# Softmax over 16384 rows: row maxima taken out of the main path, and two late loads moved to another queue

## The chip, the cores and the metric

The kernel runs on one core of a Trainium2 chip. The metric is device time in microseconds (us). The profile's span runs from the first to the last instruction and is some 1.3 to 1.6 us shorter than the device time.

## The reference, cut to what matters

```python
x: float32 [16, 1024, 512], standard normal
x_scaled = x / 2.0
exp_x = exp(x_scaled - max(x_scaled, axis=-1))
out = exp_x / sum(exp_x, axis=-1)
```

That is 16384 softmaxes over 512 values. Input and output are 33.55 MB each. A "row" below is one 512-value row of each of the 128 partitions, 0.262 MB; there are 128 of them.

## The kernel before

Ten tiles of 3, 7, 13 and seven times 15 rows share an SBUF arena of 98 rows, so tiles 8 and 9 must wait until earlier tiles are stored.

```python
# loads: tile 0 on SyncE's queue, tiles 1 to 7 on ScalarE's, all issued at once
nc.sync.dma_start(out=sb(0), in_=dram(xf, 0))                   # t == 0
for p, q, lo, hi in ((0, P, 0, r), (0, 126, r, r + 1), (126, P, r, r + 1)):   # t == 1
    nc.scalar.dma_start(out=sb(t)[p:q, lo:hi], in_=dram(xf, t)[p:q, lo:hi])
...
# VectorE, chunk k (3 to 5 rows): maxima, and two chunks behind them the division
nc.vector.reduce_max(out=stats[...], in_=arena[...], negate=True)._wait_ge(ld[t], ...)
nc.vector.reciprocal(out=recip[...], in_=stats[...])._wait_ge(s_exp, k + 1)
nc.vector.tensor_mul(...)                       # tiles 1 to 3: one per chunk
nc.vector.tensor_scalar_mul(...)                # other tiles: one per row
...
# ScalarE, per row: waits for the chunk's maxima
nc.scalar.activation(out=arena[:, a + r], in_=arena[:, a + r], func=Exp,
    bias=stats[:, b + r : b + r + 1], scale=0.5, accum_out=stats[:, b + r : b + r + 1])
... # after the exponentials of tiles 4 and 5: the late loads, on ScalarE's queue
nc.scalar.wait_ge(*need[u]); nc.scalar.dma_start(out=sb(u), in_=dram(xf, u))   # u = 8, 9
...
# SyncE: the stores, in order
for t in range(len(tiles)):
    nc.sync.wait_ge(s_mul, last_chunk[t] + 1)
    nc.sync.dma_start(out=dram(of, t), in_=sb(t))
```

## Time and profile before

| | before |
|---|---|
| time, median of 3 runs | 160.1 us (160.06 to 160.21) |
| span of the profiled run | 158.6 us |
| VectorE busy | 131.4 us, 83% |
| ScalarE busy | 94.4 us, 60% |
| two DMA queues, share of 16 engines | 50.6% and 48.5% |

Besides the lines that the prediction shows, these are the page's costliest groups of the kernel before. The columns are line, engine, operation, operands, count; then busy us and mean ns; then the idle time ahead of them and what ended it.

```profile
L118 DVE TENSOR_REDUCE stats<-arena 128x5 f32<-128x2560 f32 (+2 forms) x27 | 72.2, 2676 | 14.6 <-DMA arena<-in_x_dram 14.6
L176 ACT ACTIVATE arena<-arena,stats 128x512 f32<-128x512 f32 x68 | 48.2, 710 | 23.4 <-DVE stats L118 23.4
L138 DVE TENSOR_SCALAR arena<-arena,recip 128x512 f32<-128x512 f32 x93 | 38.6, 482 | 0.7
L131 DVE TENSOR_TENSOR arena<-arena,recip 128x2560 f32<-128x2560 f32 (+2 forms) x8 | 19.9, 2491 | 0.3
```

The first line is the whole cost of the row maxima: more than half of VectorE's busy time. The second shows ScalarE waiting 23.4 us for them.

### The profile page before, as it was taken

How to read it: one execution, taken by the hardware profiler on the slowest of the kernel's cores; microseconds unless marked ns; L12 is line 12 of the kernel's file. 1: busy time of each engine (PE TensorE's matmuls, PEld its weight loads, DVE VectorE, ACT ScalarE, POOL GpSimd, SP SyncE). 2: the span in 40 equal slices, each digit the busy share in tenths (PEclk: the TensorE clock that was granted, in tenths of full speed). 3: DMA queues.
4: the chain of work that ended last, by engine and by line, in shares of the span. 5: the costliest groups of instructions: out<-in, count | busy, mean ns of one | idle time of the engine just before them, and what ended most of it. 6: DMA issues, size and time to landing. Idle time of an engine off the chain costs nothing.

```text
span 158.6 us, 621 instructions
## 1 busy us (share of the span) xinstructions
DVE 131.4 (83%) x155; ACT 94.4 (60%) x257; POOL 0.2 (0%) x4
## 2 busy tenths in 40 slices
DVE  0466799999999999999999999996999389999000
ACT  0369197736874594669738797666566809763000
POOL 0000000000000000000000000000000000000000
DMA  7999999999999999999999999999999999999996
GB/s 268 449 373 430 414 431 466 435 407 399 466 443 389 434 463 448 418 444 426 442 426 434 426 426 442 426 441 411 457 395 472 395 473 395 472 395 465 395 472 263
DMA packets 3026, 67.13 MB, mean 423 GB/s; under 512 B 336, under 2 KB 336, under 8 KB 720
## 3 DMA queue, kind: packets, MB, share of 16 engines
q1 hardware_dynamic: 1584, 34.34, 50.6%
q10 hardware_dynamic: 1440, 32.77, 48.5%
q14 instruction: 2, 0.02, 0.0%
HBM read 33.55 MB, written 33.55 MB: 423 GB/s over the span
## 4 chain that ended last, share of the span: by engine, by line
DMA 52%; DVE 38%; issue 0%
DMA arena<-in_x_dram 38%; DVE stats L118 18%; DMA out_dram<-arena 14%; DVE arena L131 13%; DVE arena L138 7%; DVE recip L127 1%
## 5 line engine op out<-in xcount | busy, mean ns | idle before, releaser
L118 DVE TENSOR_REDUCE stats<-arena 128x5 f32<-128x2560 f32 (+2 forms) x27 | 72.2, 2676 | 14.6 <-DMA arena<-in_x_dram 14.6
L176 ACT ACTIVATE arena<-arena,stats 128x512 f32<-128x512 f32 x68 | 48.2, 710 | 23.4 <-DVE stats L118 23.4
L211 ACT ACTIVATE arena<-arena,stats x60 | 42.5, 710 | 20.7 <-ACTq L203 20.7
L138 DVE TENSOR_SCALAR arena<-arena,recip 128x512 f32<-128x512 f32 x93 | 38.6, 482 | 0.7
L131 DVE TENSOR_TENSOR arena<-arena,recip 128x2560 f32<-128x2560 f32 (+2 forms) x8 | 19.9, 2491 | 0.3
L176 ACT ACTIVATION_READ_ACCUMULATOR arena<-arena,stats 128x1 f32 x68 | 12.7, 187 | 0.0
L211 ACT ACTIVATION_READ_ACCUMULATOR arena<-arena,stats x60 | 11.2, 187 | 0.0
L127 DVE RECIPROCAL recip<-stats 128x5 f32<-128x5 f32 (+2 forms) x27 | 4.8, 177 | 0.0
L171 ACT ACT_TABLE_LOAD x1 | 1.3, 1283 | 5.7 <-issue 5.7
L252 POOL MEMSET const-bfloat16-1.0<- 128x1 bf16 x1 | 0.1, 101 | 0.0
L252 POOL MEMSET const-uint8-127<- 128x1 uint8 x1 | 0.1, 101 | 0.0
L252 POOL MEMSET const-float32-0.0<- 128x1 f32 x1 | 0.1, 98 | 0.2 <-issue 0.2
L252 POOL MEMSET const-float32-1.0<- 128x1 f32 x1 | 0.1, 98 | 0.0
## 6 DMA issues: line engine op xcount, KB each, us to landing
arena<-in_x_dram ACTq DMA_DIRECT2D x7, 3840.0 KB, 46.6
out_dram<-arena SPq DMA_DIRECT2D x7, 3840.0 KB, 22.7
arena<-in_x_dram ACTq DMA_DIRECT2D x1, 3328.0 KB, 14.3
out_dram<-arena SPq DMA_DIRECT2D x1, 3328.0 KB, 21.1
out_dram<-arena SPq DMA_DIRECT2D x1, 1792.0 KB, 18.2
arena<-in_x_dram ACTq DMA_DIRECT2D x1, 1536.0 KB
arena<-in_x_dram SPq DMA_DIRECT2D x1, 768.0 KB, 6.2
out_dram<-arena SPq DMA_DIRECT2D x1, 768.0 KB, 15.8
```

What stands on the lines that cost most here:

```text
L118: nc.vector.reduce_max(out=stats[:, b : b + c], in_=arena[:, a : a + c], axis=mybir.AxisListType.X, negate=True,)._wait_ge(ld[t], 48 if t ...
L127: nc.vector.reciprocal(out=recip[:, b : b + c], in_=stats[:, b : b + c])._wait_ge(s_exp, k + 1).then_inc(s_rec, 1)
L131: nc.vector.tensor_mul(out=arena[:, a : a + c], in0=arena[:, a : a + c], in1=recip[:, b : b + c].unsqueeze(2).to_broadcast([P, c, D]),)._w ...
L138: ins = nc.vector.tensor_scalar_mul(out=arena[:, a + r], in0=arena[:, a + r], scalar1=recip[:, b + r : b + r + 1],)
L171: nc.scalar.preload_act_table(mybir.ActivationFunctionType.Exp)
L176: ins = nc.scalar.activation(out=arena[:, a + r], in_=arena[:, a + r], func=mybir.ActivationFunctionType.Exp, bias=stats[:, b + r : b + r ...
L211: ins = nc.scalar.activation(out=data, in_=data, func=mybir.ActivationFunctionType.Exp, bias=stat, scale=0.5, accum_out=stat,)
L252: nc = _bacc.Bacc("TRN2", target_bir_lowering=False, num_devices=1)
```

## The change

The intent is to relieve VectorE: exponentials of x/2 without the maximum subtracted are safe for ordinary data, so the main path drops the maxima, checks at its end that all 16384 sums lie between 1 and 1e30, and otherwise computes everything again in a general path with maxima, whose DMAs GpSimd issues. The two late loads go to SyncE's queue, between stores. Two smaller parts go along: the divisions become 18 products of up to ten rows, and ScalarE's loop takes 105 rows instead of 60.

```diff
-        nc.vector.reduce_max(out=stats[:, b : b + c], in_=arena[:, a : a + c], negate=True, ...)
...
                 ins = nc.scalar.activation(
-                    out=arena[:, a + r], in_=arena[:, a + r], func=Exp,
-                    bias=stats[:, b + r : b + r + 1], scale=0.5,
-                    accum_out=stats[:, b + r : b + r + 1],
+                    out=arena[:, b], in_=arena[:, b], func=Exp, scale=0.5,
+                    accum_out=stats[:, b : b + 1],
                 )
...
-        for r in range(c):
-            ins = nc.vector.tensor_scalar_mul(...)
+            nc.vector.tensor_mul(...)          # 18 in all, over up to 10 rows
...
-                nc.scalar.wait_ge(*need[u])
-                nc.scalar.dma_start(out=sb(u), in_=dram(xf, u)).then_inc(ld[u], 16)
...
+        for t in (0, 1, 2, 3):
+            store(nc.sync, t)
+        for t, then in ((8, (4,)), (9, (5, 6, 7, 8, 9))):
+            nc.sync.wait_ge(s_home[t], landings(LATE[t]))
+            load(nc.sync, t)
+            for u in then:
+                store(nc.sync, u)
...
+        nc.vector.tensor_scalar(out=inside[:, :], in0=stats[:, :], scalar1=LO, scalar2=HI, ...)
+        ...                                    # compare, count, 1x1 matmul, flag
+        rounds(nc.vector, vector)              # general path, skipped when the flag says so
+        rounds(nc.scalar, scalar)
+        rounds(nc.gpsimd, gpsimd, n_rows // G)
```

More of the change, by code (lines that the diff above doesn't have):

```diff
@@ L6 @@
 from concourse._compat import with_exitstack
-PLAN = [
-    ([3], 0), ([4, 3], 3), ([5, 4, 4], 10), ([5] * 3, 23), ([5] * 3, 38), ([5] * 3, 53),
-    ([5] * 3, 68), ([5] * 3, 83), ([5] * 3, 0), ([5] * 3, 15),
+TILES = [
+    (3, 0), (7, 3), (13, 10), (15, 23), (15, 38), (15, 53), (15, 68), (15, 83), (15, 0), (15, 15),
 ]
+LATE = {8: (0, 1, 2), 9: (3,)}
 ARENA = 98
-LAG = 2
+HEAD = [3, 4, 3, 5, 4, 4]
+E = 5
 SPREAD = 1
-AFTER = {8: 4, 9: 5}
-FUSED = {1, 2, 3}
-LOOP = 6
-E = 5
+LO, HI = 1.0, 1.0e30
+G = 8
 @with_exitstack
@@ L38 @@
     fp32 = mybir.dt.float32
+    Exp = mybir.ActivationFunctionType.Exp
+    Alu = mybir.AluOpType
     xf = x.flatten_outer_dims()
@@ L44 @@
     n_rows = N // P
-    assert sum(sum(c) for c, _ in PLAN) == n_rows
+    assert sum(r for r, _ in TILES) == n_rows
     arena = nc.alloc_sbuf_tensor("arena", (P, ARENA, D), fp32)
@@ L50 @@
     recip = nc.alloc_sbuf_tensor("recip", (P, n_rows), fp32)
-    tiles, chunks, base = [], [], 0
-    for t, (cs, at) in enumerate(PLAN):
-        r = sum(cs)
+    inside = nc.alloc_sbuf_tensor("inside", (P, n_rows), fp32)
+    count = nc.alloc_sbuf_tensor("count", (P, 1), fp32)
+    ones = nc.alloc_sbuf_tensor("ones", (P, 1), fp32)
+    flag = nc.alloc_sbuf_tensor("flag", (1, 1), mybir.dt.int32)
+    g_max = nc.alloc_sbuf_tensor("g_max", (P, G), fp32)
+    g_sum = nc.alloc_sbuf_tensor("g_sum", (P, G), fp32)
+    total = nc.alloc_psum_tensor("total", (1, 1), fp32)
+    tiles, base = [], 0
+    for r, at in TILES:
+        assert at == base % ARENA
         tiles.append((base, r, at))
-        o = 0
-        for c in cs:
-            chunks.append((t, base + o, c, at + o))
-            o += c
         base += r
-    last_chunk = {c[0]: k for k, c in enumerate(chunks)}
     def dram(ap, t):
@@ L71, in sb @@
         return arena[:, at : at + r, :]
-    behind = {}
-    for t, (_, r, at) in enumerate(tiles):
-        for u in range(t):
-            _, ru, au = tiles[u]
-            if at < au + ru and au < at + r:
-                behind.setdefault(t, []).append(u)
-    ld = [nc.alloc_semaphore(f"ld{t}") for t in range(len(tiles))]
-    awaited = sorted({u for us in behind.values() for u in us})
-    st, need = {}, {}
-    for t in sorted(behind):
-        new = [u for u in behind[t] if u not in st]
-        sem = nc.alloc_semaphore(f"st{t}")
-        st.update({u: sem for u in new})
-        need[t] = (sem, 16 * len(new))
+    straight = sum(HEAD)
+    sizes = HEAD + [E] * ((n_rows - straight) // E)
+    starts = [sum(sizes[:k]) for k in range(len(sizes))]
+    assert sum(sizes) == n_rows
+    owner = [max(t for t, (b, _, _) in enumerate(tiles) if b <= s) for s in starts]
+    assert all(s + c <= sum(tiles[t][:2]) for s, c, t in zip(starts, sizes, owner))
+    pairs = []
+    for k, t in enumerate(owner):
+        if pairs and len(pairs[-1]) == 1 and owner[pairs[-1][0]] == t:
+            pairs[-1].append(k)
+        else:
+            pairs.append([k])
+    upto = [1 + max(j for j, ks in enumerate(pairs) if owner[ks[0]] == t) for t in range(len(tiles))]
+    ld = [nc.alloc_semaphore(f"ld{t}") for t in range(len(tiles))]
+    s_home = {t: nc.alloc_semaphore(f"s_home{t}") for t in LATE}
     s_end = nc.alloc_semaphore("s_end")
-    s_max = nc.alloc_semaphore("s_max")
     s_exp = nc.alloc_semaphore("s_exp")
@@ L96 @@
     s_mul = nc.alloc_semaphore("s_mul")
-    def issue_loads(begin, end):
-        for t in range(begin, end):
-            if t in behind:
-                continue
-            if t == 0:
-                nc.sync.dma_start(out=sb(t), in_=dram(xf, t)).then_inc(ld[t], 16)
-            elif t == SPREAD:
-                r = tiles[t][1] - 1
-                for p, q, lo, hi in ((0, P, 0, r), (0, 126, r, r + 1), (126, P, r, r + 1)):
-                    nc.scalar.dma_start(
-                        out=sb(t)[p:q, lo:hi], in_=dram(xf, t)[p:q, lo:hi]
-                    ).then_inc(ld[t], 16)
-            else:
-                nc.scalar.dma_start(out=sb(t), in_=dram(xf, t)).then_inc(ld[t], 16)
@@ L116, in do_max @@
-    def do_max(k):
-        t, b, c, a = chunks[k]
-        nc.vector.reduce_max(
-            out=stats[:, b : b + c],
-            in_=arena[:, a : a + c],
-            axis=mybir.AxisListType.X,
-            negate=True,
-        )._wait_ge(ld[t], 48 if t == SPREAD else 16).then_inc(s_max, 1)
-    def do_mul(k):
-        t, b, c, a = chunks[k]
-        nc.vector.reciprocal(
-            out=recip[:, b : b + c], in_=stats[:, b : b + c]
-        )._wait_ge(s_exp, k + 1).then_inc(s_rec, 1)
-        if t in FUSED:
+    s_ones = nc.alloc_semaphore("s_ones")
@@ new lines, with load @@
+    s_cnt = nc.alloc_semaphore("s_cnt")
+    s_tot = nc.alloc_semaphore("s_tot")
+    s_flag = nc.alloc_semaphore("s_flag")
+    g_ld = nc.alloc_semaphore("g_ld")
+    g_go = nc.alloc_semaphore("g_go")
+    g_st = nc.alloc_semaphore("g_st")
+    g_neg = nc.alloc_semaphore("g_neg")
+    g_exp = nc.alloc_semaphore("g_exp")
+    g_rec = nc.alloc_semaphore("g_rec")
+    g_mul = nc.alloc_semaphore("g_mul")
+    def load(eng, t):
+        r = tiles[t][1]
+        parts = [(0, P, 0, r)]
+        if t == SPREAD:
+            parts = [(0, P, 0, r - 1), (0, 126, r - 1, r), (126, P, r - 1, r)]
+        for p, q, lo, hi in parts:
+            eng.dma_start(
+                out=sb(t)[p:q, lo:hi], in_=dram(xf, t)[p:q, lo:hi]
+            ).then_inc(ld[t], 16)
@@ new lines, with landings, store @@
+    stored_by = {u: s_home[t] for t, us in LATE.items() for u in us}
+    for t, (_, r, at) in enumerate(tiles):
+        over = {u for u, (_, ru, au) in enumerate(tiles[:t]) if at < au + ru and au < at + r}
+        assert over <= {u for v, us in LATE.items() if v <= t for u in us}
+    def landings(ts):
+        return 16 * len(list(ts))
+    at_end = landings(t for t in range(len(tiles)) if t not in stored_by)
+    def store(eng, t):
+        eng.wait_ge(s_mul, upto[t])
+        eng.dma_start(out=dram(of, t), in_=sb(t)).then_inc(stored_by.get(t, s_end), 16)
@@ new lines, in take, with rounds, early, loads @@
+    def take(eng, sem, n):
+        eng.wait_ge(sem, n).then_inc(sem, -n)
+    def rounds(eng, body, step=1):
+        last = n_rows // G
+        i = eng.alloc_register("tile")
+        eng.wait_ge(s_flag, 1)
+        eng.reg_load(i, flag[0:1, 0:1])
+        with eng.While(lambda: eng.snap(i, min_val=0, max_val=last) < last):
+            body(eng.snap(i, min_val=0, max_val=last - 1))
+            eng.reg_add(i, i, step)
+    def early():
+        load(nc.sync, 0)
+        load(nc.scalar, 1)
+    def loads():
+        for t in range(2, min(LATE)):
+            load(nc.scalar, t)
@@ L131, in do_mul, with program @@
+    def program():
+        nc.vector.memset(ones[:, :], 1.0).then_inc(s_ones, 1)
+        for j, ks in enumerate(pairs):
+            b, c = starts[ks[0]], sum(sizes[k] for k in ks)
+            a = b % ARENA
+            nc.vector.reciprocal(
+                out=recip[:, b : b + c], in_=stats[:, b : b + c]
+            )._wait_ge(s_exp, ks[-1] + 1).then_inc(s_rec, 1)
             nc.vector.tensor_mul(
@@ L134, in do_mul @@
                 in1=recip[:, b : b + c].unsqueeze(2).to_broadcast([P, c, D]),
-            )._wait_ge(s_rec, k + 1).then_inc(s_mul, 1)
-            return
-        for r in range(c):
-            ins = nc.vector.tensor_scalar_mul(
-                out=arena[:, a + r],
-                in0=arena[:, a + r],
-                scalar1=recip[:, b + r : b + r + 1],
-            )
-            if r == 0:
-                ins._wait_ge(s_rec, k + 1)
-        ins.then_inc(s_mul, 1)
-    def compute_and_store():
-        for k in range(len(chunks) + LAG):
-            if k < len(chunks):
-                do_max(k)
-            if k >= LAG:
-                do_mul(k - LAG)
-        for t in range(len(tiles)):
-            nc.sync.wait_ge(s_mul, last_chunk[t] + 1)
-            nc.sync.dma_start(out=dram(of, t), in_=sb(t)).then_inc(
-                st[t] if t in awaited else s_end, 16
-            )
-        nc.sync.wait_ge(s_end, 16 * (len(tiles) - len(awaited)))
-        straight = [k for k, c in enumerate(chunks) if c[0] < LOOP]
-        loop = [k for k, c in enumerate(chunks) if c[0] >= LOOP]
-        for k in loop:
-            nc.tensor.wait_ge(s_max, k + 1).then_inc(s_go, 1)
-        nc.scalar.preload_act_table(mybir.ActivationFunctionType.Exp)
-        late = sorted(behind)
-        for k in straight:
-            t, b, c, a = chunks[k]
-            for r in range(c):
-                ins = nc.scalar.activation(
-                    out=arena[:, a + r],
-                    in_=arena[:, a + r],
-                    func=mybir.ActivationFunctionType.Exp,
-                    bias=stats[:, b + r : b + r + 1],
-                    scale=0.5,
-                    accum_out=stats[:, b + r : b + r + 1],
-                )
-                if r == 0:
-                    ins._wait_ge(s_max, k + 1)
@@ new lines, in program @@
+            )._wait_ge(s_rec, j + 1).then_inc(s_mul, 1)
+        nc.vector.tensor_scalar(
+            out=inside[:, :], in0=stats[:, :], scalar1=LO, scalar2=HI,
+            op0=Alu.max, op1=Alu.min,
+        ).then_inc(s_cnt, 1)
+        nc.vector.tensor_tensor(
+            out=inside[:, :], in0=inside[:, :], in1=stats[:, :], op=Alu.is_equal
+        )._wait_ge(s_cnt, 1).then_inc(s_cnt, 1)
+        nc.vector.reduce_sum(
+            out=count[:, :], in_=inside[:, :], axis=mybir.AxisListType.X
+        )._wait_ge(s_cnt, 2).then_inc(s_cnt, 1)
@@ new lines, in program @@
+        nc.vector.tensor_scalar(
+            out=flag[:, :], in0=total[:, :], scalar1=float(N), scalar2=float(n_rows // G),
+            op0=Alu.is_ge, op1=Alu.mult,
+        )._wait_ge(s_tot, 1).then_inc(s_flag, 1)
+        for t in range(len(tiles)):
+            nc.tensor.wait_ge(ld[t], 48 if t == SPREAD else 16).then_inc(s_go, owner.count(t))
+        nc.tensor.wait_ge(s_ones, 1)
+        nc.tensor.matmul(
+            total[:, :], lhsT=count[:, :], rhs=ones[:, :], start=True, stop=True
+        )._wait_ge(s_cnt, 3).then_inc(s_tot, 1)
@@ L186, in compute_and_store @@
+        nc.scalar.preload_act_table(Exp)
+        for k, c in enumerate(HEAD):
+            take(nc.scalar, s_go, 1)
+            for b in range(starts[k], starts[k] + c):
+                ins = nc.scalar.activation(
+                    out=arena[:, b], in_=arena[:, b], func=Exp, scale=0.5,
+                    accum_out=stats[:, b : b + 1],
+                )
             ins.then_inc(s_exp, 1)
-            while late and last_chunk[AFTER[late[0]]] <= k:
-                u = late.pop(0)
-                nc.scalar.wait_ge(*need[u])
-                nc.scalar.dma_start(out=sb(u), in_=dram(xf, u)).then_inc(ld[u], 16)
@@ L191, in compute_and_store @@
-        assert not late
-        first = chunks[loop[0]][1]
-        assert all(
-            c == E and b == first + j * E and a == b % ARENA
-            for j, (_, b, c, a) in enumerate(chunks[k] for k in loop)
-        )
-        row = nc.scalar.alloc_register("row")
+        exponentials(straight, n_rows)
+        for t in (0, 1, 2, 3):
[5 more added lines that the diff above has]
+                store(nc.sync, u)
@@ new lines, in program, with vector @@
+        x_g = xf.rearrange("(t p r) d -> t p r d", p=P, r=G)
+        o_g = of.rearrange("(t p r) d -> t p r d", p=P, r=G)
+        data = arena[:, 0:G]
+        def vector(i):
+            take(nc.vector, g_go, 1)
+            nc.vector.reduce_max(
+                out=g_max[:, :], in_=data, axis=mybir.AxisListType.X, negate=True
+            ).then_inc(g_rec, 1)
+            take(nc.vector, g_rec, 1)
+            nc.vector.tensor_scalar_mul(
+                out=g_max[:, :], in0=g_max[:, :], scalar1=0.5
+            ).then_inc(g_neg, 1)
+            take(nc.vector, g_exp, 1)
+            nc.vector.reciprocal(out=g_sum[:, :], in_=g_sum[:, :]).then_inc(g_rec, 1)
+            take(nc.vector, g_rec, 1)
+            nc.vector.tensor_mul(
+                out=data, in0=data, in1=g_sum[:, :].unsqueeze(2).to_broadcast([P, G, D])
+            ).then_inc(g_mul, 1)
@@ new lines, in scalar, with gpsimd @@
+        def scalar(i):
+            take(nc.scalar, g_neg, 1)
+            for r in range(G):
+                ins = nc.scalar.activation(
+                    out=arena[:, r], in_=arena[:, r], func=Exp, scale=0.5,
+                    bias=g_max[:, r : r + 1], accum_out=g_sum[:, r : r + 1],
+                )
+            ins.then_inc(g_exp, 1)
+        def gpsimd(_):
+            nc.gpsimd.wait_ge(s_end, at_end)
+            for i in range(n_rows // G):
+                nc.gpsimd.dma_start(out=data, in_=x_g[i]).then_inc(g_ld, 16)
+                nc.gpsimd.wait_ge(g_ld, 16 * (i + 1)).then_inc(g_go, 1)
+                take(nc.gpsimd, g_mul, 1)
+                nc.gpsimd.dma_start(out=o_g[i], in_=data).then_inc(g_st, 16)
+                nc.gpsimd.wait_ge(g_st, 16 * (i + 1))
@@ L200, in compute_and_store, with exponentials @@
+        rounds(nc.vector, vector)
+        rounds(nc.scalar, scalar)
+        rounds(nc.gpsimd, gpsimd, n_rows // G)
+        nc.sync.wait_ge(s_end, at_end)
+    def exponentials(first, end):
+        row = nc.scalar.alloc_register(f"row{first}")
         nc.scalar.reg_mov(row, first)
-        with nc.scalar.While(lambda: nc.scalar.snap(row, min_val=first, max_val=n_rows) < n_rows):
-            now = nc.scalar.snap(row, min_val=first, max_val=n_rows - E)
-            nc.scalar.wait_ge(s_go, 1).then_inc(s_go, -1)
+        with nc.scalar.While(lambda: nc.scalar.snap(row, min_val=first, max_val=end) < end):
+            now = nc.scalar.snap(row, min_val=first, max_val=end - E)
+            take(nc.scalar, s_go, 1)
@@ L209, in compute_and_store @@
                 data = arena[:, r : ARENA - E + 1 + r][:, bass.ds(at, 1)]
-                stat = stats[:, r : n_rows - E + 1 + r][:, bass.ds(now, 1)]
                 ins = nc.scalar.activation(
-                    out=data,
-                    in_=data,
-                    func=mybir.ActivationFunctionType.Exp,
-                    bias=stat,
-                    scale=0.5,
-                    accum_out=stat,
+                    out=data, in_=data, func=Exp, scale=0.5,
+                    accum_out=stats[:, r : n_rows - E + 1 + r][:, bass.ds(now, 1)],
                 )
@@ L228 @@
     nc.switch_bb("main", None)
-    issue_loads(0, 2)
+    early()
     first = list(entry.instructions)
@@ L235 @@
     nc.switch_body(here, parent=None, valid_engines=[i.engine for i in jumps])
-    issue_loads(2, len(tiles))
-    compute_and_store()
+    loads()
+    program()
 _INS = ['x']
```

## The prediction

> **What bounds the kernel now.** I read the page from the top: the DMA row and the queue table first, because the kernel does little arithmetic per byte, then the chain, then the costliest groups.
>
> ```profile
> span 158.6 us, 621 instructions
> DVE 131.4 (83%) x155; ACT 94.4 (60%) x257; POOL 0.2 (0%) x4
> ...
> DMA  7999999999999999999999999999999999999996
> ...
> q1 hardware_dynamic: 1584, 34.34, 50.6%
> q10 hardware_dynamic: 1440, 32.77, 48.5%
> ...
> HBM read 33.55 MB, written 33.55 MB: 423 GB/s over the span
> ...
> DMA 52%; DVE 38%; issue 0%
> ```
>
> Two readings compete. VectorE is busy 83% and holds 38% of the chain, so it looks like a partner in the bound. But the DMA row has a 9 in every slice but the first and the last, and the two queues' packets took 50.6% + 48.5% = 99.1% of what 16 engines can do in 158.6 us, which is 157.2 us. The packet records of the trace say the same: the first payload packet starts at 1.00 us, the last ends at 158.19 us, and 158.19 - 1.00 = 157.2 us. So the DMA engines have no hole at all between their first and last byte. The DVE pieces of the chain are the releaser of a store at that moment, but other transfers were moving meanwhile.
>
> The rate in stretches of the span, by window (columns: stretch, its length, busy us of DVE, ACT and POOL with instruction counts, TensorE clock, DMA share, GB/s):
>
> ```profile
> 2.00:10.00 8.00, 2.48 (x2) 3.27 (x6) 0.00 (x0) 1.00 1.03 403
> 10.00:58.00 48.00, 45.32 (x30) 31.47 (x89) 0.00 (x0) 1.00 1.02 435
> 58.00:106.00 48.00, 47.65 (x66) 34.23 (x95) 0.00 (x0) 1.00 1.00 431
> 106.00:147.00 41.00, 35.95 (x59) 25.45 (x70) 0.00 (x0) 1.00 1.00 432
> 147.00:157.00 10.00, 0.00 (x0) 0.00 (x0) 0.00 (x0) 1.00 1.01 436
> ```
>
> From 10 us on the rate is 431 to 436 GB/s whether VectorE is nearly always busy (58 to 106) or idle (147 to 157), and whether loads and stores mix or only stores are left. Only the head is slower (403). A packet of 30720 B, one partition's share of a 15-row tile, takes 1138 ns in the median on either queue: 27.0 GB/s per engine, 432 for 16.
>
> The wait view of SyncE's queue shows the slack at the end:
>
> ```profile
> SPq L158 <- DVE arena L138: 98.1, 7, 17.8
> SPq L162 <- DMA out_dram<-arena: 11.3, 1, 11.3
> ```
>
> SyncE waits 98.1 us for VectorE's products, which costs nothing while the load queue has work. After the last store is issued (146.98 us) it still waits 11.3 us: at 432 GB/s that is 4.9 MB, the last 3.93 MB store and 1 MB of the one before it. Its packets start at 148.41, 0.7 us before those of the store ahead end (149.11), so there is no hole and an earlier product would not have helped.
>
> [...] the 7-row store (14336 B packets) beside loads of 30720 B moved 1.835 MB from 30.40 to 43.12 us, 144 GB/s or 33% of 432, where 14336/(14336+30720) is 32%. [...]
>
> **The change part by part.** In rows (one row of all 128 partitions is 0.262 MB, 0.607 us at 432 GB/s; a 15-row tile 9.1 us alone, 18.2 us at half share).
>
> *Removed:* 27 row-maximum reductions, 72.2 us of VectorE, and with them ScalarE's waits on them (23.4 us in the straight part and most of the 20.7 us in the loop). None of it separates the first byte from the last, so directly 0 us. The DMA bytes, tiles and packet sizes are the same: 128 rows in, 128 out, so again 157 us of packets.
>
> *Swapped:* 93 tensor_scalar (38.6 us) and 8 tensor_tensor (19.9) become 18 tensor_tensor over up to 10 rows. [...] with 18 reciprocals at 0.18 (3.2 us) VectorE falls from 131 to about 75 us. ScalarE keeps 128 exponentials at 0.71 us pitch.
>
> *Order:* the stores start earlier. Tile 0 lands at 6.2, ScalarE is free of its table load at 7.0, three exponentials end near 9.2, the 3-row product (1.76) near 11.3, so store 0 issues 3.3 us earlier than 14.65. Tile 1 lands at 9.3: seven exponentials to 14.3, a 7-row product (3.9) to 18.5, against 26.3 before. Tile 2: landed by about 18, thirteen exponentials to 28, store near 32, against 41.75. The earlier stores take share from the loads, which therefore land later; the sum of the two rates is unchanged.
>
> *Late loads:* tiles 8 and 9 now go on SyncE's queue behind store 3 and store 4. I worked the queues through with the packet shares (estimates from the numbers above). ScalarE's queue lands tiles 3, 4, 5, 6, 7 near 31, 48, 66, 84 and 102. A tile's store is ready some 16 us after landing: 15 exponentials 10.9, then the last 5-row product 3.0 and small waits. SyncE's queue then holds: store 2 33 to 50, store 3 (issued 47) 50 to 68, load 8 (needs stores 0 to 2, issued about 52) 68 to 86, store 4 (issued 64) 86 to 103, load 9 (needs store 3, issued about 70) 103 to 112 at the full rate, because the other queue is empty from 102. What remains is five stores of 9.1 us: 112, 121, 130, 139, 148 are their starts and 157 to 158 the end. They are ready at 82, 100, 118, 129 (tile 8 after tile 7 on ScalarE) and 140 (tile 9). The tightest has 8 us to spare; a store's first packet can come up to 3.7 us after its issue (store 0: 14.65 to 18.33), so count 4. No hole opens after the load queue runs dry.
>
> *Added:* a memset, four small VectorE operations, a 1x1 matmul, flag reads on three engines. They follow the last product at about 140 and take a few us (estimate), inside the 17 us until the last byte lands. The sums of exponentials of normal data are some hundreds, between 1 and 1e30, so the general path is skipped.
>
> Sum: 0 from VectorE, 0 from bytes, a few tenths either way from the head. Of the 157.2 us of packets, 67.11 MB at 432 GB/s explain 155.3; the other 1.9 is mostly in the first 10 us, whose loads the change keeps. From span to time is 1.5 us now (160.1 - 158.6). Predicted 160.0 us.
>
> **Rivals.** *VectorE was the bound:* with 72 us removed, the chain's 38% would suggest a gain of several us. For it: 83% busy and the chain. Against: no hole in the DMA. Even removing every loss, 155.3 of bytes + 1.0 head + 0.4 tail + 1.5 leaves 158.2, so faster by 2% (156.9) is out of reach. *Starvation:* SyncE blocks on landings before loads 8 and 9 and cannot issue ready stores meanwhile; load and store share one ring, so the last 55 us have a single queue. For it: a single point of order, and loads that land up to 12 us later than before (tile 7: 102 against 89.85). Against: those 4 to 8 us of spare and 433 GB/s of a lone queue from 147 to 157. If tile 7 or the last products came 12 us later than I worked out, it would cost 4 us or more: 164. *Overhead at the ends:* GpSimd's DMAs are only in the unused path, but the flag reads and the extra queue could cost about 1 us outside the span: 161. *A smoother mix:* fewer small packets mixed with large ones in the first 60 us could win 0.5: 159.5.
>
> **Range and chances.** Overhead is likelier to add than the head to give, so the range is 159.2 to 161.3 around 160.0. Faster by over 2% contradicts the byte count: 1%. Slower by over 2% needs 3.2 us of holes, against 4 to 8 us of spare: 4%. Within 2%: 95%.
>
> **What the profile should show.** The reductions gone, VectorE near 75 us and 47% busy; the DMA row still 9s; queue shares still summing to 99% but moved from 50.6/48.5 to about 62/37 (SyncE has 161 rows of 256); first store near 11.5; last product near 140, with SyncE's final wait grown from 11.3 to some 17 us; windows of 431 to 436 GB/s throughout. The prediction is wrong if a slice after the first has a DMA digit under 9, if the general path runs, or if the time outside the span grows past 1.5 us.

## The result, and the profile after

| | before | after |
|---|---|---|
| time, median | 160.08 us (159.96 to 160.21, 4 runs) | 160.61 us (160.33 to 160.90, 4 runs) |
| span of the profiled run | 158.6 us | 159.1 us |
| VectorE busy | 131.4 us | 74.9 us |
| ScalarE busy | 94.4 us | 80.5 us |

The ratio is 1.0033 with a 95% interval of 1.0013 to 1.0053. Ratios here are the mean time of one kernel's fast runs over that of the other's in the same rounds, so they are not quite the ratio of the medians quoted. VectorE lost 56 us of work, and the kernel became 0.3% slower: the same within 2%, as predicted.

The page of the changed kernel:

```profile
span 159.1 us, 624 instructions
...
PE 0.2 (0%) x2; PEld 0.1 (0%) x2; DVE 74.9 (47%) x41; ACT 80.5 (51%) x257; POOL 0.2 (0%) x4
...
DMA  7999999999999999898999999999999999999996
...
q1 hardware_dynamic: 1872, 42.21, 62.0%
q10 hardware_dynamic: 1152, 24.90, 36.9%
...
DVE 6%; issue 1%; ACT 1%; PE 0%; ACTq 0%
...
L269 ACT ACTIVATE arena<-arena x105 | 64.4, 613 | 35.6 <-ACTq L132 26.7
L163 DVE TENSOR_TENSOR arena<-arena,recip 128x5120 f32<-128x5120 f32 (+5 forms) x18 | 71.1, 3951 | 0.6
L160 DVE RECIPROCAL recip<-stats 128x10 f32<-128x10 f32 (+5 forms) x18 | 3.6, 197 | 54.7 <-ACT arena L269 40.0
```

The packets of the two queues still fill the 16 engines: 62.0 + 36.9 = 98.9% of 159.1 us, 157.4 us, as 99.1% of 158.6 was 157.2. What moved is the split between the queues: SyncE's, q1, carries the two late loads beside all stores, 42.21 MB instead of 34.34. The one-line chain (DVE 6%) shows a trap: it follows the last instruction back through the check of the sums, which ended at 133 us, and so says nothing of the transfers that filled the last 26 us. Before, the same part of the page named DMA 52%, though that chain too ended early, with the last product at 147 us. The chain alone could not have been compared from one kernel to the other.

The DMA row has two digits of 8, which the prediction had named as a sign against itself. Two adjacent windows around the first of them (columns: stretch, length, busy us of PE, PEld, DVE, ACT and POOL with counts, clock, DMA share, GB/s):

```profile
63.60:67.60 4.00, 0.00 (x0) 0.00 (x0) 0.00 (x0) 4.00 (x15) 0.00 (x0) 1.00 0.91 392
67.60:71.60 4.00, 0.00 (x0) 0.00 (x0) 2.88 (x2) 4.00 (x14) 0.00 (x0) 1.00 1.10 476
```

A share of 1.10 cannot be a busy share, so it must come from how whole packets of 1.14 us are credited to a slice; the pair together has 434 GB/s. Packet by packet, sharing each over the slices that it spans, every 2 us stretch from 2 to 156 us comes out busy to 100% within 2%. There is no hole; the sign was badly chosen.

The same stretches as the prediction showed of the kernel before, in the changed kernel (columns as above):

```profile
10.00:58.00 48.00, 0.00 (x0) 0.00 (x0) 27.97 (x15) 30.60 (x100) 0.00 (x0) 1.00 1.02 434
58.00:106.00 48.00, 0.00 (x0) 0.00 (x0) 20.16 (x11) 25.79 (x83) 0.00 (x0) 1.00 1.00 431
106.00:147.00 41.00, 0.19 (x2) 0.09 (x2) 25.84 (x15) 20.45 (x68) 0.00 (x0) 1.00 1.00 430
147.00:157.00 10.00, 0.00 (x0) 0.00 (x0) 0.00 (x0) 0.00 (x0) 0.00 (x0) 1.00 1.00 433
```

The work of VectorE in the second stretch fell from 47.65 to 20.16 us, and the rate stayed at 431 GB/s. What VectorE saved turned up as its own waiting: 40 us more ahead of its work on a chunk (54.7 us in the line of L160 above, where L118 had 14.6 before), and most of the rest after its last instruction, 26 us to the end instead of 12. The waits of SyncE's queue only changed places:

```profile
SPq L129 <- DVE arena L163: 101.1, 10, 17.9
SPq L255 <- DMA out_dram<-arena: 26.6, 1, 26.6
SPq L113 <- DMA out_dram<-arena: 24.5, 2, 14.0
```

They sum to 152.2 us; before, two lines on VectorE (98.1 and 43.1) and the last wait (11.3) summed to 152.5. The last store is issued 26.6 us before everything has landed, against 11.3 us before. The third line is the new wait ahead of the two late loads; ScalarE's queue still had loads during it (until 97 us; the second late load was issued at 74.4), so it cost nothing.

### The profile page after: what moved, and what is told of

It reads as the page before. It is cut to its first block, busy times and chain, and to the rows that moved or that the text cites. A ratio compares the mean times of both kernels' runs of the same rounds, so it can differ in the third digit from the quotient of the medians.

```text
span 159.1 us, 624 instructions
## 1 busy us (share of the span) xinstructions
PE 0.2 (0%) x2; PEld 0.1 (0%) x2; DVE 74.9 (47%) x41; ACT 80.5 (51%) x257; POOL 0.2 (0%) x4
## 3 DMA queue, kind: packets, MB, share of 16 engines
q1 hardware_dynamic: 1872, 42.21, 62.0%
q10 hardware_dynamic: 1152, 24.90, 36.9%
## 5 line engine op out<-in xcount | busy, mean ns | idle before, releaser
L269 ACT ACTIVATE arena<-arena x105 | 64.4, 613 | 35.6 <-ACTq L132 26.7
L163 DVE TENSOR_TENSOR arena<-arena,recip 128x5120 f32<-128x5120 f32 (+5 forms) x18 | 71.1, 3951 | 0.6
L160 DVE RECIPROCAL recip<-stats 128x10 f32<-128x10 f32 (+5 forms) x18 | 3.6, 197 | 54.7 <-ACT arena L269 40.0
L269 ACT ACTIVATION_READ_ACCUMULATOR arena<-arena x105 | 19.5, 186 | 0.0
L195 ACT ACTIVATE arena<-arena 128x512 f32<-128x512 f32 x23 | 14.1, 615 | 4.6 <-ACTq L132 4.5
L195 ACT ACTIVATION_READ_ACCUMULATOR arena<-arena 128x1 f32 x23 | 4.3, 187 | 0.0
```

What stands on the lines that cost most here:

```text
L160: nc.vector.reciprocal(out=recip[:, b : b + c], in_=stats[:, b : b + c])._wait_ge(s_exp, ks[-1] + 1).then_inc(s_rec, 1)
L163: nc.vector.tensor_mul(out=arena[:, a : a + c], in0=arena[:, a : a + c], in1=recip[:, b : b + c].unsqueeze(2).to_broadcast([P, c, D]),)._w ...
L195: ins = nc.scalar.activation(out=arena[:, b], in_=arena[:, b], func=Exp, scale=0.5, accum_out=stats[:, b : b + 1],)
L269: ins = nc.scalar.activation(out=data, in_=data, func=Exp, scale=0.5, accum_out=stats[:, r : n_rows - E + 1 + r][:, bass.ds(now, 1)],)
```

## The experiments

Theory: the 16 DMA engines bind both kernels from the first byte to the last, and the order of loads and stores matters only where it opens a hole. Rivals: VectorE was part of the bound and something new ate the gain (the general path, the late loads' queue); or the maxima were never worth anything anywhere.

**The changed kernel again.** No edit.

> The changed kernel unaltered, to place its small loss beside the other runs of this call. Theory A (the 0.3% is real and belongs to the program): 160.4 to 160.8 us against 160.1 of before, ratio 1.002 to 1.005. Theory B (chance of one chip or one call): ratio 1.000 within 0.001.

Measured: 160.46 us (160.27 to 160.59), before in the same rounds 160.17; ratio 1.0018 (1.0006 to 1.0031). The loss repeats, at about half its first size. The ratio lies just under what theory A allowed (1.002 to 1.005) and above theory B's (1.001 at most), but its interval takes in both; the first call's interval does not reach B's.

**No general path.**

```diff
-        nc.vector.tensor_scalar(out=inside[:, :], ...)     # and compare, count, flag
-        nc.tensor.matmul(total[:, :], lhsT=count[:, :], rhs=ones[:, :], ...)
-        rounds(nc.vector, vector)
-        rounds(nc.scalar, scalar)
-        rounds(nc.gpsimd, gpsimd, n_rows // G)
```

> The changed kernel without the check of the sums, the flag and the general path (no GpSimd DMA, no matmul). If the general path costs the 0.5 us (its code, its extra queue, its flag reads at the end): back to 160.1 us. If it lies beside the last stores, as predicted: as after_again, within 0.2 us. Every slower engine is done near 132 us in both.

Measured: 160.17 us (160.00 to 160.59), ratio 1.0009 (0.9996 to 1.0022). The intervals of the two runs overlap, so the ratios alone do not tell them apart. The split of each run into span and rest does. Mean span: 158.93 us without the general path, 158.88 with it, 158.85 for the kernel before, all the same. Mean time less span: 1.32 us without, 1.54 with it, 1.34 before (1.61 in the first four runs of the changed kernel). So about 0.2 us lies after the last instruction of the span, and in the trace one instruction fetch follows the end there (160.42 us, where the span ended at 159.09); the traces of the kernel before and of this run have none.

**Which engine's skipped code is it?**

```diff
-        rounds(nc.gpsimd, gpsimd, n_rows // G)
```

> The changed kernel without GpSimd's part of the general path alone (its 32 unrolled DMAs and its flag read). The general path seems to add 0.2 us outside the span (time less span 1.54 to 1.61 us with it, 1.32 without), where one instruction fetch follows the end. If that is GpSimd's code: time less span back to 1.34 and no fetch after the end. If it is VectorE's or ScalarE's skipped loop: still 1.55 to 1.6 us and the fetch at about the end plus 1.3 us.

Measured: 160.51 us (160.25 to 160.81), ratio 1.0026 (1.0012 to 1.0040); time less span 1.62 us, and the fetch still comes after the end, at 160.10 us with the span's end at 158.77. It is not GpSimd's code nor its DMAs. Three more kernels with a general path, met below, had their last fetch before the end of the span (142 us of 159, 153 of 159, 162 of 166) and times less span of 1.38, 1.31 and 1.35 us, like kernels without it. So the cost goes with where the fetch falls, in all thirteen kernels that were traced: time less span is 1.52 to 1.62 us in the six with a fetch behind the last instruction, 1.31 to 1.38 us in the seven without. That the fetch is its cause is not shown, and which of the other engines fetches, and why, is open.

**Late loads back on ScalarE's queue.** The first 68 rows of exponentials are written out again to make room for the issues.

```diff
+            for t, behind in ((8, 4), (9, 5)):     # on ScalarE, after the chunk that ends tile 4 / 5
+                if k + 1 == len(owner) - owner[::-1].index(behind):
+                    nc.scalar.wait_ge(s_home[t], landings(LATE[t]))
+                    load(nc.scalar, t)
...
-        for t in (0, 1, 2, 3): ...                 # SyncE: stores only, in order
+        for t in range(len(tiles)):
+            store(nc.sync, t)
```

> The changed kernel with the two late loads moved back to ScalarE's queue (issued after the exponentials of tiles 4 and 5, as before). If the order on SyncE's queue costs the 0.5 us (a lone queue from 97 us on, loads and stores in one ring): 160.1 us. If only bytes count: as after_again within 0.2 us; the queue shares go back to near 50 and 48%.

Measured: 162.78 us (161.47 to 163.11), ratio 1.0136 (1.0103 to 1.0169). Both expectations were wrong, and this is the most telling run. Its timeline, VectorE's last two products (start, length, instruction), and below it the window around the end of the second (columns as before):

```profile
141.72 5.49 DVE L163 TENSOR_TENSOR arena<-arena,recip 128x5120 f32<-128x5120 f32 x1
...
147.34 2.83 DVE L163 TENSOR_TENSOR arena<-arena,recip 128x2560 f32<-128x2560 f32 x1
```

```profile
147.00:152.00 5.00, 0.19 (x2) 0.09 (x2) 3.99 (x7) 0.00 (x0) 0.00 (x0) 1.00 0.47 203
```

The last store was issued at 150.2 us, and the packets of the store ahead ended at 149.45: DMA stood still for 1.6 us until 151.03, and 203 GB/s stand where the kernel before has 436. The packet records show how it came. Without maxima the stores start earlier (the second one's packets at 25.25 instead of 30.40 us) and take rate from the loads: a 15-row load took 18.5 us beside running stores, where the last store, alone, took 9.9. Tile 9's packets then end at 133.38 us, against 126.17 before and 113.32 in the changed kernel. From there to the end of the last product ScalarE and VectorE need 16.8 us instead of 20.8, which does not make up the 7.2 us.

Another part of the change has a share in these 16.8 us. ScalarE was done with the last five rows at 144.5 us, but their product waited until 147.34 for the ten-row product ahead of it. So this run is not the removal of the maxima alone: no run has the maxima removed, the loads left where they were and products of five rows. (Two of the six runs took 161.5 us, four 162.8 to 163.1; the profile is of one of the slower.)

**The same, with the end cut finer**, to see whether the hole is the whole loss.

```diff
-        if pairs and len(pairs[-1]) == 1 and owner[pairs[-1][0]] == t:
+        if t != 9 and pairs and len(pairs[-1]) == 1 and owner[pairs[-1][0]] == t:
...
+        for j in range(3):                         # the last tile: three stores of 5 rows
+            nc.sync.wait_ge(s_mul, upto[9] - 2 + j)
+            nc.sync.dma_start(out=dram(of, 9)[:, 5 * j : 5 * j + 5], in_=sb(9)[:, 5 * j : 5 * j + 5])
```

> The kernel of e2_late_on_scalar (late loads on ScalarE's queue, 162.8 us) with the products and the store of the last tile cut into three pieces of 5 rows. If its loss is the 1.6 us hole ahead of the last store (tile 9 lands at 133.4, its whole product is done at 150.2): the first piece is ready near 140 us, the hole closes, 160.4 to 160.8 us. If the loss is the cost of two mixed queues: still 162 to 163 us.

Measured: 160.41 us (160.22 to 160.81), ratio 1.0012 (0.9997 to 1.0026). The first piece was issued at 140.50 us, its packets follow those of the store ahead without a gap, and 2.4 us come back. The loss was the hole, not the mixing of queues. The last product here (start, length):

```profile
143.77 2.83 DVE L163 TENSOR_TENSOR arena<-arena,recip 128x2560 f32<-128x2560 f32 x1
```

It ends 14.2 us after tile 9's last packet (132.42 us), not 16.8. With that, the run before would have had its whole last tile multiplied at 147.6 us, and its packets some 1.4 us later (as in the kernel before), at 149.0 instead of 151.03. By this estimate most of the hole comes from the ten-row product; a run with five-row products and one whole store would have to show it.

**Only the late loads moved, in the kernel before.**

```diff
-                nc.scalar.wait_ge(*need[u])
-                nc.scalar.dma_start(out=sb(u), in_=dram(xf, u)).then_inc(ld[u], 16)
+            u = {4: 8, 5: 9}.get(t)                # SyncE, ahead of stores 4 and 5
+            if u is not None:
+                nc.sync.wait_ge(*need[u])
+                nc.sync.dma_start(out=sb(u), in_=dram(xf, u)).then_inc(ld[u], 16)
```

> The kernel before with only the late loads moved to SyncE's queue between stores 3, 4 and 5. VectorE no longer waits 1.4 and 3.3 us for tiles 8 and 9, so its last product comes near 142 us instead of 147. If that end mattered: 4 us faster. If DMA is the bound: 160.1 to 160.6 us, no hole, SyncE's last wait longer by some 5 us.

Measured: 160.29 us (160.10 to 160.58), ratio 1.0007 (0.9994 to 1.0020). SyncE's last wait grew from 11.3 to 16.6 us, as expected: the last product came some 5 us sooner, and the time did not move.

```profile
SPq L166 <- DMA out_dram<-arena: 16.6, 1, 16.6
```

The new order of the loads thus cost nothing measurable beside the old maxima, with VectorE busy 131.2 us.

**Half of the stores left out, in both kernels** (wrong results: the second half of each tile's rows is never written).

```diff
-        eng.dma_start(out=dram(of, t), in_=sb(t)).then_inc(stored_by.get(t, s_end), 16)
+        half = tiles[t][1] // 2
+        eng.dma_start(out=dram(of, t)[:, :half], in_=sb(t)[:, :half]).then_inc(stored_by.get(t, s_end), 16)
```

> Wrong on purpose: the kernel before, storing only the first half of each tile's rows (59 rows of 128). DMA then has 187 rows of 0.607 us, 114 us. My theory (before is DMA-bound with VectorE close under it): VectorE binds, about 6 + 131 + 4 of waits + a 7-row store, 146 to 151 us. If DMA alone ever mattered: about 117 us.

> Wrong on purpose: the changed kernel with the same half stores. My theory: the removed reductions now pay, because VectorE (75 us) and ScalarE (81 us) are both under DMA's 114 us: 116 to 124 us, some 28 us under the same cut of the kernel before. Rival (removing the maxima is worth nothing anywhere, because engines only wait on each other): within 5 us of that cut.

Measured: 149.13 us for the kernel before (149.07 to 149.34) and 125.17 us for the changed one (124.49 to 125.29). Chain and DMA row of the kernel before with half stores:

```profile
DMA  7999999989999999899999999970820082008237
...
DVE 84%; DMA 10%; issue 0%
```

Now VectorE binds, and DMA has holes from about 100 us on (slice 27, counted from 0, of 3.7 us); in this setting the whole change is worth 24 us. So VectorE's work does cost time, only not where DMA has 67 MB to move (160.08 and 160.61 us). How much of the 24 us the maxima alone account for was not run. The changed kernel came out 1 us above its range: its last tile is multiplied too late (last store issued at 117.58, the packets of the store ahead end at 113.71), so a hole of 4.7 us opens there too.

**The freed VectorE time filled again.**

```diff
+            nc.vector.reduce_max(out=ballast[:, b : b + c], in_=arena[:, a : a + c], negate=True)
             nc.vector.reciprocal(...)
```

> The changed kernel with 18 reductions over all 128 rows put back on VectorE as ballast (results unused), ahead of each reciprocal: some 147 us of VectorE. If only bytes count: as after_again, 160.6 us. My theory: the margin of the last store (ready at 132 us, first packet at 148.5) is eaten, because tiles 7, 8 and 9 are all multiplied after tile 7 lands at 97 us: 97 + 6.5 + 3 times 17 = 154.5, store 9 from there 9.1 us and some latency, so about 166 us with a hole before the last store.

Measured: 167.41 us (167.35 to 167.85), ratio 1.0455 (1.0440 to 1.0470). The timeline of the last product (start, length), and the window around it:

```profile
152.45 2.83 DVE L168 TENSOR_TENSOR arena<-arena,recip 128x2560 f32<-128x2560 f32 x1
```

```profile
147.00:157.00 10.00, 0.19 (x2) 0.09 (x2) 9.11 (x8) 0.00 (x0) 0.00 (x0) 1.00 0.26 111
```

The store ahead ends at 150.03 and the last one begins at 156.13: a hole of 6.1 us, as the arithmetic of the expectation had it (which was 1.4 us short of the time). With the loads in the new order three tiles are multiplied after the last load of ScalarE's queue. But this is not the old kernel put back. The reduction stands behind the exponentials, not ahead of them, and VectorE is busy 143.6 us, 12 more than before, because the products kept their new form (71.1 us, where the old two forms took 38.6 and 19.9). With the old VectorE work the same order opened no hole (160.29 us above). So the run shows that the margin of the last store can be used up, not that the new order needs the maxima gone.

**A bias operand given back to the exponentials.**

```diff
-                    out=arena[:, b], in_=arena[:, b], func=Exp, scale=0.5,
+                    out=arena[:, b], in_=arena[:, b], func=Exp, scale=0.5,
+                    bias=zeros[:, b : b + 1],      # in the loop: bias=stat, accum_out=stat
```

> The changed kernel with a bias operand given back to the exponentials, of value zero: the first 23 rows take it from a separate column of zeros, the 105 rows of the loop from the same stats column that receives their sum (as in the kernel before). If a bias that changes from row to row costs the 97 ns (710 against 613 ns): both groups go to about 710. If it is the sharing of one column by bias and sum: the first 23 stay at 615, the loop goes to 710. The time stays at 160.5 us either way, ScalarE being busy 51%.

Measured once: 160.48 us (a single run, so of unknown state). The groups of instructions (columns as on the page):

```profile
L276 ACT ACTIVATE arena<-arena,stats x105 | 74.1, 707 | 28.2 <-ACTq L134 20.6 <-PEq L189 7.5
L200 ACT ACTIVATE arena<-arena,zeros 128x512 f32<-128x512 f32 x23 | 16.3, 709 | 3.4 <-ACTq L134 3.4
```

Both groups go back to 707 and 709 ns, where the changed kernel has 613 and 615 ns. So it is the bias operand itself, not the column shared with the sum: 94 ns for a row of 512 values.

**Tile 1 in one load.** Both kernels load the last row of tile 1 in two pieces, of 126 and of 2 partitions, which is the uneven load meant here.

```diff
-SPREAD = 1
+SPREAD = None
```

> The changed kernel with tile 1 loaded by one DMA of 128 partitions instead of three. [...] If that uneven share balances slower engines: slower by up to 0.7 us (8 packets of 84 ns), the last packets more spread. If it only adds overhead: up to 0.3 us faster, 160.3 us.

Measured: 161.17 us (160.69 to 161.76), ratio 1.0071 (1.0054 to 1.0087), by the ratios 0.6 to 0.8 us above the changed kernel. In its trace the last payload packet ends at 159.15 us, against 158.72 and 158.32 in the two profiled runs of the changed kernel. (The last 16 packets of the changed kernel ended between 157.57 and 158.72 us, those of the kernel before between 157.48 and 158.19.) The uneven load helps, but that it balances slower engines is not shown; the next run speaks against it.

**One head tile of 10 rows.**

```diff
-TILES = [(3, 0), (7, 3), (13, 10), ...]
+TILES = [(10, 0), (13, 10), ...]
-SPREAD = 1
+SPREAD = None
```

> An attempt to beat both kernels: the changed kernel with its first two tiles (3 and 7 rows, four load DMAs of 2048 to 12288 B packets) merged into one 10-row tile with 20480 B packets. The small packets of the head took about 0.8 us more per engine than their bytes at 27 GB/s would (0.52 + 0.20 + 0.09 us for the 6144, 12288 and 2048 B packets). If the small packets cause that: up to 0.8 us faster than the changed kernel, 159.7 us, which is the most that the head has to give. If it is the start-up of the DMA engines, or if the uneven third DMA of tile 1 is needed as e8_no_spread showed: 160.5 to 161.2 us.

Measured: 160.33 us (160.19 to 160.75), ratio 1.0022 (1.0008 to 1.0035). The packets did become cheaper, 156.90 us per engine instead of 157.42, but the time is within the noise of the changed kernel's. It has no uneven load and does not suffer from that. No version beat the kernel before.

## Why the prediction was right, point by point

- **DMA binds from first to last byte: right.** The rate is 430 to 434 GB/s after 10 us with VectorE at 75 instead of 131 us, and the two half-store runs show what happens when the bytes go: 149.1 and 125.2 us.
- **Removed and swapped VectorE work, 75 us: right**, 74.9 us measured. The 75 us was the estimate. It can be had from the trace before: products of 3, 4 and 5 rows took 1757, 2291 and 2825 ns there, 534 ns for each row more, from which 128 rows in 18 products take about 71 us (an estimate; 71.1 us was measured).
- **"ScalarE keeps 128 exponentials at 0.71 us pitch": wrong in size.** An exponential without the bias operand took 613 ns; the prediction carried over the length of one with it. It touched nothing on the path.
- **The queues worked through by hand: right in order, mis-sized in time.** ScalarE's queue landed tiles 3 to 7 at 29, 43, 61, 79 and 97 us where 31 to 102 was estimated, store 0 was issued at 11.06 us, the last product was done at 132.1 instead of 140. Two terms give 9.5 us: the last load of ScalarE's queue, 5 us sooner, and 45 exponentials at 0.1 us less, 4.5 us. Some 2.6 us went the other way, as the last five-row product waited for a ten-row product (123.67 to 129.16 us), which its sum had left out. With the last product, the last store was issued sooner, so SyncE's final wait was 26.6 us and not 17.
- **"No hole opens": right**, with more room than said: last store issued at 132.14, first packet needed at 148.49. "The sum of the two rates is unchanged" holds while both queues have work (434 GB/s from 10 to 58 us, 435 in the kernel before). The prediction checked the one order that it was given. It did not ask what the order is worth: with the loads left on ScalarE's queue the earlier stores delay the last load by 7 us and, with the ten-row product, a hole opens (162.8 us).
- **Rival "overhead at the ends": happened, at a quarter of its size.** It was put at 1 us, the author's estimate; 0.2 us appeared outside the span, and not from GpSimd's DMAs. The check of the sums, a few us by estimate, took 1.3 us (132.04 to 133.33 us) and lay beside the last stores. The time outside the span also was 1.34 us in the mean before, not the 1.5 us that came from subtracting the profiled run's span from the median of others.
- **Its own signs of being wrong: two of three came up.** The digits of 8 were a matter of how slices are credited. The time outside the span did pass 1.5 us (1.61 in the first, 1.54 in the second); that sign was real, and worth 0.2 to 0.27 us. The general path did not run: VectorE's 41 instructions are the memset, 18 reciprocals, 18 products and the 4 of the check.
- **What is left of the 0.5 us.** The first showed 0.5, the second 0.3. Of that 0.2 to 0.27 us is outside the span. The rest is 0.03 us of mean span in the second. In the first it is some 0.26 us (an estimate, since the spans of the kernel before were not kept there), where mean spans of the kernel before differ by 0.13 us from call to call (158.72 to 158.85). It stays open.

## What to carry to other kernels

Add up what the DMA queues' packets took, as a share of all engines' time, before believing a busy engine or a chain: at the 99% of this kernel, 56 us less work on VectorE did not bring the end forward (160.08 and 160.61 us), and what VectorE saved became waiting. In such a kernel ask of each change whether the queues could run dry. With the late loads on ScalarE's queue the earlier stores took rate from the later loads, the last of them ended at 133.38 instead of 126.17 us, and DMA stood still for 1.6 us ahead of the last store (162.78 us); that hole closed when the last tile's product and store were cut into pieces (160.41 us). When a run puts work back, compare the engine's busy time with that of the kernel before: here 12 us more came back than had been taken away (143.6 against 131.4 us).
